# First expert's tokens chosen alone on token-major scores, the others' inside the expert stage; modulation sums on VectorE; new pads in the expert pool

## The chip, the core and the metric

One core of a Trainium2 chip runs the kernel. The metric is the device time of one execution in microseconds; it is the median of several executions. PE is the TensorE matmul queue, PEld its weight loads, DVE is VectorE, ACT is ScalarE, POOL is GpSimd and SP is SyncE, which here only issues DMAs.

## The reference

One layer of a transformer block on 2048 tokens of width 1024, in float32. What the change touches:

```python
mod = silu(c) @ w_ada + b_ada                 # 6 rows of 1024: sh1, sc1, g1, sh2, sc2, g2
h = ln(x) * (1 + sc1) + sh1                   # modulated input
y = token_mixer(h @ w_in, ...)                # convolution branch + two-way retention, gated, @ w_out
x = layer_norm(ALPHA * x + g1 * y)
h = ln(x) * (1 + sc2) + sh2
aff = softmax(h @ w_router)                   # 2048 tokens x 16 experts
gates, idx = top_k(aff.T, 256)                # each expert takes its 256 best tokens
xe = h[idx]                                   # 16 x 256 x 1024
he = silu(xe @ w_gate) * (xe @ w_up)
ye = (he @ w_down) * gates                    # added back at idx
x = layer_norm(ALPHA * x + g2 * sum(ye))
```

## The kernel before

All products are float32 by three matmuls: each operand is split into a rounded high part and the rest (`split`, lines 78 to 85: ACT makes the high part at L80, DVE, or POOL on request, subtracts at L81), and `mm3` (L87 to L89) multiplies high by high, high by low and low by high. Raw weights come by DMA into four "raw" buffers of 512 KB, and the split weights stand in a ring of 24 "w" slots.

The program runs in stages. First the modulation rows sh1 and sc1 are made (`first_modulation`), then the in-projection goes in two halves of the tokens over groups of output columns (U, K, Q, V, G, GA, GB), with the 31-tap convolution on DVE as a filler (`cacc`, L466). Then come retention, the mixing of the two branches with the router (`affs`, the 2048 x 16 scores, made at L860), the choice of each expert's tokens, and 16 experts. An expert has four steps f2 of gate and up products (32 products of 128x256 in each step) and then 32 down products of 128x512.

**Modulation.** `ada_rows` (L237) makes sc2, sh2, g1 and g2 from 1024x1024 pieces of `w_ada`: `ada_k` puts plain float32 matmuls (L199) of a 32-column stationary `crep` on PE. Rounds 0 and 1 (g1, sh2; sc2) are a generator that `fillers2` pumps, one step after each pair of token tiles of half 0 from group 6 on (`pump(1, fillers2)`). Round 2 (g2) is pumped between the counts of the search (`g2fill`); its two 2 MB loads (`wg2`, L929) borrow the places of the expert tiles heT and xeT.

**Search.** The scores are transposed so that each expert has 8 partitions of 256 tokens (`seg`). All 16 thresholds are then found together, two bits a round, in 15 rounds: three compares with counting on DVE (L953), a matmul that adds up the 8 partitions (L956), and two small steps (L967, L971). Ties and ranks follow (L981 to L1006, ending in `pin`, each token's place in each expert's list), then expert 0's list by one-hot products (L1040 to L1058, `idx`), its gather on POOL (`x_gather`, L1075), the transposes and splits of its 256 token rows (`x_prep`), and the lists of experts 0 to 3 (`make_lists(0)`, matmuls `ix` at L1024).

**What sets the order.** A scheduler orders each engine's queue by the place in the program and by its own estimates; `tc.issue_after` ties a step to an instruction. The weights of expert 0's first three steps (`first`, L914) are loaded and split ahead, with the subtraction on POOL. Within the expert stage the gather of expert e+1 stands at the start of expert e and its `x_prep` after step f2 = 1. Two small tiles `pad0` and `pad1` (24 and 8 floats, L927) stand ahead of heT and xeT in the pool.

Of the kernel before, what the change touches and what calls it, by code (L numbers as in the profile page):

```python
# [42 lines left out]
def body(ctx: ExitStack, tc: tile.TileContext, x, ctxt, cc, w_ada0, w_ada, b_row, b_col, w_in, conv_w, conv_b,  # L43
         conv_g, conv_bb, w_conv, lgf, lgb, gn_g, w_ret, w_out, ln1_g, ln1_b, w_router,
         w_gate, w_up, w_down, ln2_g, ln2_b, k_rope, k_pos, k_dif, k_sel, k_iota, k_bits, out):
# [144 lines left out]
    def ada_k(crep, c0, ps, k, halves=2, pre=None):  # L190
        for half in range(halves):
            if pre is not None:
                wt = pre[k // 4][:, k % 4]
            else:
                wt = raw(f"wa{c0}_{k}_{half}", [P, D])
                nc.sync.dma_start(wt, w_ada[c0 // D - 2 + half, k])
            for j in range(2):
                jj = half * 2 + j
                T.matmul(ps[32 * jj:32 * jj + 32, :], crep[:, k], wt[:, j * 512:(j + 1) * 512],  # L199
                         start=k == 0, stop=k == KD - 1)  # L200
                if pre is not None:
                    yield
        if pre is None:
            yield

# [31 lines left out]
    def ada_rows(crep, rnd, halves, tmp, pre=None):  # L237
        c0 = 2048 * (rnd + 1) if rnd < 2 else 5120
        n = 2 * halves

        def load_b():
            br = tmp("br")
            for j in range(n):
                nc.sync.dma_start(br[32 * j:32 * j + 32], bass.AP(tensor=b_row.tensor, offset=b_row.offset + c0 + 512 * j,
                                                                  ap=[[0, 32], [1, 512]]))
            return br

        ps = u_ps(f"ada{rnd + 1}")
        br = load_b() if pre is not None else None
        for k in range(KD):  # L250
            yield from ada_k(crep, c0, ps, k, halves, pre)
        mr = tmp("mr")
        if br is None:
            br = load_b()
        V.tensor_tensor(mr[:32 * n], ps[:32 * n], br[:32 * n], ALU.add)
        for j in range(n):
            r = c0 // 512 - 4 + j
            nc.sync.dma_start(d_mod[r:r + 1], mr[32 * j:32 * j + 1])
        yield
# [412 lines left out]
    for half in range(2):  # L672
        pairs = [half * 4 + i for i in range(4)]
        for gi, g in enumerate(GROUPS):
# [5 lines left out]
            for pi, pid in enumerate(plist):  # L680
# [107 lines left out]
    digit = const.tile([P, 15, 4], I32, name="digit")  # L788
    nc.scalar.dma_start(digit, k_bits)
    sameb = const.tile([P, P], BF16, name="sameb")  # L790
    kst = r2k("kst")
    nc.scalar.dma_start(kst[:, :P], k_sel[:, 1])
    V.tensor_copy(sameb, kst[:, :P])
# [113 lines left out]
    iota16, tokid, blk, iota128 = kio[:, 0:16], kio[:, 16:32], kio[:, 32:40], kio[:, 40:168]  # L907
# [16 lines left out]
    same, low = ksel[:, 0], ksel[:, 1]  # L924
    wg2 = []
# [4 lines left out]
    g2fill = [ada_rows(rep_c(ep)[0], 2, 1, lambda name: e4k(name, [P, 512]), wg2)]  # L930
    with tc.issue_after(pows[0].ins), tc.issue_after(exps[0].ins):
        first = [[gu_slabs(w[0], f2, True) for w in (w_gate, w_up)] for f2 in range(3)]
    segb = e2k("seg")
    seg = segb[:, :256]
    ps = tr_ps()
    for a in range(2):
        T.transpose(ps[:, a * P:(a + 1) * P], affs[:, a].rearrange("p s e -> p (s e)"), ident)
    V.tensor_copy(seg, ps[:, :256])
    seg16 = ep.tile([P, 256], BF16, name="seg16", tag="tk_seg16", bufs=1)
    V.tensor_copy(seg16, seg.bitcast(BF16).rearrange("p (n two) -> p n two", two=2)[:, :, 1])  # L940

    dps = mm_ps("dps").bitcast(I32)
    digp = dps[:, 0:60].rearrange("p (i c) -> p i c", c=4)
    nxp = dps[:, 64:124].rearrange("p (i c) -> p i c", c=4)
    V.tensor_copy(dps[:, 0:60], digit.rearrange("p i c -> p (i c)"))
    cand = tk("cand", 4, I32, 2)
    V.tensor_copy(cand, digp[:, 14])
    for i in range(14, -1, -1):
        cnt = tk("cnt", 3, BF16, 2)
        for j in range(3):  # L950
            junk = e2k("junk")
            junk = junk[:, :128].bitcast(BF16) if i >= 8 else junk[:, :256]
            V.tensor_scalar(junk, seg16 if i >= 8 else seg, cand[:, j + 1:j + 2].bitcast(F32), 0.0,  # L953
                            op0=ALU.is_ge, op1=ALU.add, accum_out=cnt[:, j:j + 1])
        pc = u_ps("cnt")
        cmm = T.matmul(pc[:, 0:3], sameb, cnt, start=True, stop=True)  # L956
        if i < 14:
            with tc.issue_after(cmm.ins):
                pump(1, g2fill)
        hits = tk("hits", 3, F32, 2)  # L960
        dig = tk("dig", 1, F32, 2)
        if i > 0:
            nx = nxp[:, i]
            V.tensor_tensor(nx, cand[:, 0:1].to_broadcast([P, 4]), digp[:, i - 1], ALU.bitwise_or)
        else:
            nx = cand[:, 0:1].to_broadcast([P, 4])
        V.tensor_scalar(hits, pc[:, 0:3], CAP - 0.5, 0.0, op0=ALU.is_ge, op1=ALU.add, accum_out=dig)  # L967
        cand = tk("cand", 4, I32, 2)
        if i >= 4:

            V.scalar_tensor_tensor(cand, dig.to_broadcast([P, 4]), float(1 << 2 * i), nx, op0=ALU.mult, op1=ALU.add)  # L971
        else:
            digi = tk("digi", 1, I32, 2)
            V.tensor_scalar(digi, dig, float(1 << 2 * i), None, op0=ALU.mult)
            V.tensor_tensor(cand, digi.to_broadcast([P, 4]), nx, ALU.bitwise_or)
    tb = cand[:, 0:1]
    thr = tb.bitcast(F32)
    ge = e2k("ge")
    gt, eq = ge[:, :256], ge[:, 256:]
    cc2 = tk("cc2", 2)  # L980
    V.tensor_scalar(gt, seg, thr, 0.0, op0=ALU.is_gt, op1=ALU.add, accum_out=cc2[:, 0:1])  # L981
    V.tensor_scalar(eq, seg, thr, 0.0, op0=ALU.is_equal, op1=ALU.add, accum_out=cc2[:, 1:2])
    pc = u_ps("cnt")
    T.matmul(pc[:, 0:1], same, cc2[:, 0:1], start=True, stop=True)
    T.matmul(pc[:, 1:2], low, cc2[:, 1:2], start=True, stop=True)
    lim = tk("lim", 1)
    V.tensor_scalar(lim, pc[:, 0:1], -1.0, float(CAP), op0=ALU.mult, op1=ALU.add)
    V.tensor_tensor(lim, lim, pc[:, 1:2], ALU.subtract)
    oneb = e2k("oneb")
    ones, scn = oneb[:, :256], oneb[:, 256:]  # L990
    V.memset(ones, 1.0)
    V.tensor_tensor_scan(scn, ones, eq, 0.0, op0=ALU.mult, op1=ALU.add)
    selb = e2k("selb")
    sel, sq = selb[:, :256], selb[:, 256:]
    V.scalar_tensor_tensor(sq, scn, lim, eq, op0=ALU.is_le, op1=ALU.mult)
    cs1 = tk("cs1", 1)
    V.scalar_tensor_tensor(sel, gt, 1.0, sq, op0=ALU.mult, op1=ALU.add, accum_out=cs1)
    pc = u_ps("cnt")
    T.matmul(pc[:, 0:1], low, cs1, start=True, stop=True)
    V.tensor_tensor_scan(scn, ones, sel, 0.0, op0=ALU.mult, op1=ALU.add)  # L1000
    V.scalar_tensor_tensor(sq, scn, pc[:, 0:1], sel, op0=ALU.add, op1=ALU.mult)
    ps = tr_ps()
    for a in range(2):
        T.transpose(ps[:, a * P:(a + 1) * P], sq[:, a * P:(a + 1) * P], ident)
    pin = tk("pin", 256, I32)
    V.tensor_scalar(pin, ps[:, :256], -1.0, None, op0=ALU.add)  # L1006
    def make_lists(gq):
        e0 = gq * 4
        px = u_ps("ix")
        n = 0  # L1010
        for a in range(2):
            for s0 in range(0, 8, 4):
                oa = ep.tile([P, 256], F32R, name="oa", tag="e2k", bufs=6)
                ob = ep.tile([P, 2, 256], F32R, name="ob", tag="e2k", bufs=6)
                for off, dst in ((0, oa), (256, ob[:, 0])):
                    src = pabf[:, off + a * P + s0 * NE:off + a * P + (s0 + 4) * NE].rearrange("p (s e) -> p s e", s=4)[:, :, e0:e0 + 4]
# [21 lines left out]
    pin0 = pin.rearrange("p (a s e) -> p a s e", a=2, s=8)[:, :, :, 0]  # L1038
    pt = tk("pt", 32, I32)
    V.tensor_scalar(pt[:, 0:16].rearrange("p (s a) -> p a s", a=2), pin0, P - 1, None, op0=ALU.bitwise_and)  # L1040
# [22 lines left out]
    V.tensor_scalar(pa, pin, 4, None, op0=ALU.arith_shift_right)  # L1063
    V.tensor_scalar(pb, pin, 15, None, op0=ALU.bitwise_and)
    pabf = e2k("pabf")
    V.tensor_copy(pabf, pab)

# [221 lines left out]
```

## Time and profile before

| | us |
|---|---|
| median of 3 runs | 3068.63 (3064.36 to 3070.91) |
| the profiled execution | 3070.69 |
| its span (first to last instruction) | 3068.9 |
| PE busy | 2978.8 (97%) |
| DVE busy | 2114.8 (69%) |
| ACT busy | 1158.3 (38%) |
| POOL busy | 361.2 (12%) |
| DMA | 560.25 MB, 183 GB/s |

About 1.8 us lie around the span. The profiled execution is 2.06 us above the median. Durations in what follows are of this one execution. Matmuls are pipelined, so the row of a matmul is longer than the distance to the next one: the cost of a matmul on a full PE is the distance from its start to the next start. PE's mean granted clock is 0.988 of full speed.

### The profile page before, as it was taken

Reading aid. Unit: us, or ns where it says so; the run is one execution under the profiler, and the core shown is the slowest. Engines: PE = TensorE matmul, PEld = TensorE weight load, DVE = VectorE, ACT = ScalarE, POOL = GpSimd, SP = SyncE. Lnnn points to the kernel's source line nnn. Section 1 sums busy time; section 2 is a strip of 40 time slices with the busy share of each in tenths; the row PEclk is TensorE's granted clock in tenths of the full one; section 3 lists DMA queues with packets and bytes.
Section 4 is the critical chain, followed back from the end, with each engine's and each line's share of the span. In section 5 each row is a group of like instructions: output and inputs, shape, how many; then the busy total and the mean of one; then the engine's idle time right before and its main releaser. Section 6 shows DMA issues by size and latency. Waiting matters only on the chain. (4 is left out here: it accounts for less than half of the span.)

```text
span 3068.9 us, 47411 instructions
## 1 busy us (share of the span) xinstructions
PE 2978.8 (97%) x18089; PEld 2603.1 (85%) x18089; DVE 2114.8 (69%) x3898; ACT 1158.3 (38%) x2110; POOL 361.2 (12%) x325
## 2 busy tenths in 40 slices
PE   6999999999999999999999996999999999999998
PEld 5988877789888888888878883999999999999987
DVE  4366777442678986888867777566666666568886
ACT  4323122242231333544421112555555555544443
POOL 2100000000000000111101114010100000012331
PEclk9999999999999999999999997999999999999999
DMA  7334455332452334666764445667677667778875
GB/s 249 106 121 172 146 178 173 116 110 82 170 190 82 122 117 144 215 206 206 242 209 152 145 138 183 198 203 206 211 216 215 216 209 211 214 245 269 274 239 202
DMA packets 195044, 560.25 MB, mean 183 GB/s; under 512 B 29064, under 2 KB 44328, under 8 KB 194816
## 3 DMA queue, kind: packets, MB, share of 16 engines
q1 hardware_dynamic: 170272, 486.90, 47.8%
q0 software_dynamic: 18064, 64.62, 7.4%
q10 hardware_dynamic: 6480, 5.70, 0.6%
q8 instruction: 142, 2.33, 0.3%
q14 instruction: 86, 0.70, 0.1%
HBM read 429.24 MB, written 127.89 MB: 182 GB/s over the span
## 5 line engine op out<-in xcount | busy, mean ns | idle before, releaser
L87 PE MATMUL mm<-xeT,sg 128*128 128x256 f32 x2048 | 577.0, 282 | 0.0
L89 PE MATMUL mm<-xeT,sg 128*128 128x256 f32 x2048 | 575.6, 281 | 1.2 <-DVE sg L81 1.2
L88 PE MATMUL mm<-xeT,sg 128*128 128x256 f32 x2048 | 575.5, 281 | 0.0
L81 DVE TENSOR_TENSOR sg<-rg,sg 128x512 fp32r<-128x512 f32 x488 | 329.8, 690 | 249.2 <-ACT sg L80 244.5
L80 ACT ACTIVATE sg<-rg 128x512 fp32r<-128x512 f32 x512 | 313.5, 629 | 321.8 <-PE mm L89 222.6
L89 PEld LDWEIGHTS mm<-xeT,sg 128*128 128x128 f32 x2048 | 386.1, 189 | 1.4 <-DVE sg L81 1.4
L88 PEld LDWEIGHTS mm<-xeT,sg 128*128 128x128 f32 x2048 | 386.2, 189 | 0.7
L87 PEld LDWEIGHTS mm<-xeT,sg 128*128 128x128 f32 x2048 | 385.9, 189 | 0.7
L466 DVE SCALAR_TENSOR_TENSOR cacc<-yw,cvw,cacc 128x384 f32<-128x384 f32 (+1 forms) x600 | 376.8, 641 | 8.7
L81 DVE TENSOR_TENSOR sd<-rd,sd 128x512 fp32r<-128x512 f32 x256 | 172.6, 688 | 89.9 <-ACT sd L80 89.1
L80 ACT ACTIVATE sd<-rd 128x512 fp32r<-128x512 f32 x256 | 157.2, 629 | 135.3 <-PE mm L89 88.3
L88 PE MATMUL mm<-sd,heT 128*128 128x512 f32 x512 | 203.0, 397 | 3.7 <-DVE sd L81 3.7
L89 PE MATMUL mm<-sd,heT 128*128 128x512 f32 x512 | 203.1, 397 | 1.9 <-DVE heT L81 1.9
L87 PE MATMUL mm<-sd,heT 128*128 128x512 f32 x512 | 203.1, 397 | 1.4 <-ACT heT L80 1.4
L154 POOL TENSOR_TENSOR rs<-rs,mhalf 128x1 f32<-128x1 f32 (+1 forms) x50 | 37.6, 752 | 1294.1 <-DVE rs L153 1278.1
L87 PE MATMUL mm<-hT,sU 128*128 128x256 f32 x512 | 146.1, 288 | 4.4 <-ACT us L707 2.2
L88 PE MATMUL mm<-hT,sU 128*128 128x256 f32 x512 | 146.0, 286 | 0.0
L89 PE MATMUL mm<-hT,sU 128*128 128x256 f32 x512 | 145.1, 285 | 0.0
L147 POOL TENSOR_TENSOR rs<-rs,mhalf 128x1 f32<-128x1 f32 x58 | 86.6, 1493 | 365.9 <-DVE rs L146 365.7
L88 PEld LDWEIGHTS mm<-sd,heT 128*128 128x128 f32 x512 | 96.7, 189 | 27.4 <-DVE sd L81 5.4
L89 PEld LDWEIGHTS mm<-sd,heT 128*128 128x128 f32 x512 | 96.6, 189 | 25.9 <-DVE heT L81 3.1
L443 ACT ACTIVATE gs<-mm 128x512 f32<-128x512 f32 x96 | 54.9, 597 | 168.2 <-PE mm L89 133.0
(357 smaller groups left out, 7073.7 us busy)
## 6 DMA issues: line engine op xcount, KB each, us to landing
rg<-w_gate SPq DMA_DIRECT2D x128, 512.0 KB
rg<-w_up SPq DMA_DIRECT2D x128, 512.0 KB
rd<-w_down SPq DMA_DIRECT2D x128, 512.0 KB
wa<-w_ada SPq DMA_DIRECT2D x40, 512.0 KB
d_v<-vs SPq DMA_DIRECT2D x32, 512.0 KB
vsr<-d_v SPq DMA_DIRECT2D x32, 512.0 KB
xt<-x SPq DMA_DIRECT2D x16, 512.0 KB
rU<-w_in SPq DMA_DIRECT2D x16, 512.0 KB
```

The costliest lines, as they stand in the source:

```text
L80: A.activation(hi, src, AF.Copy)
L81: eng.tensor_tensor(lo, src, hi.bitcast(F32), ALU.subtract)
L87: T.matmul(ps, s[0], m[0], start=start, stop=False)
L88: T.matmul(ps, s[0], m[1], start=False, stop=False)
L89: return T.matmul(ps, s[1], m[0], start=False, stop=stop_)
L147: pows[0] = G.tensor_tensor(rs, rs, mhalf[:, :1], ALU.pow)
L154: G.tensor_tensor(rs[:, 0], rs[:, 0], mhalf[:, :heads], ALU.pow)
L443: A.activation(s, ps, AF.Sigmoid)
L466: V.scalar_tensor_tensor(acc[:, :n], y[:, tap:tap + n], cvw[:, cgp, tap:tap + 1], acc[:, :n], op0=ALU.mult, op1=ALU.add)
```

## The change

It has four parts.

1. `ada_rows` and `ada_k` are replaced by `ada_sums`: for each of g1, sh2, sc2 and g2, DVE multiplies 8 loaded pieces of 128x1024 by the activated conditioning vector and adds them up (8 instructions of 128x1024), then two float32 matmuls of 8x512 with `mhalf` (filled with -0.5) add over the partitions, and two small DVE steps multiply by -2 and add the bias. All four are pumped in half 0 of the in-projection, two steps after every odd pair. g2 is no longer made in the search, and the 2 MB loads there are gone.
2. `choose(e0, n, nb, ...)` replaces the common search. It works on the scores as they come out of the router, tokens on partitions, 16 of them for each expert in a partition. A round decides nb bits: one compare of 16 x n x (2^nb - 1), one reduction over the 16, one matmul with a matrix of ones, and the small steps. Expert 0 alone is searched ahead of its gather, with 4 bits a round in 8 rounds, on tiles in PSUM.
3. Experts 1 to 3 are chosen inside expert 0, 4 to 7 inside experts 1 and 2, 8 to 11 inside 3 and 4, 12 to 15 inside 5 and 6, with 3 bits a round in 10 rounds, pumped after every 6th product (expert 0) or every 16th (later). `make_lists` follows each; the gather of expert 1 comes after the first lists (f2 = 2 of expert 0), and its `x_prep` after f2 = 3.
4. The pads are now 56 and 24 floats. The constants of the search that are gone and new ones (`digit` 240 B and `sameb` 256 B out, `iota16` 64 B and `onesb` 256 B in) make the constant pool 192 bytes a partition smaller, so that all tiles behind it move. In the compiled programs the w slots, hT and most large tiles start at 0 modulo 256 bytes before and at 64 now; heT at 128 before and at 64 now; xeT at 160 before and at 96 now. Measured from the w slots, heT goes from 128 to 0 and xeT from 160 to 32.

```diff
-    def ada_k(crep, c0, ps, k, halves=2, pre=None):
...
-                T.matmul(ps[32 * jj:32 * jj + 32, :], crep[:, k], wt[:, j * 512:(j + 1) * 512],
-                         start=k == 0, stop=k == KD - 1)
-    def ada_rows(crep, rnd, halves, tmp, pre=None):
...
+    def ada_sums(c0, tmp):
+        acc = ip.tile([P, D], F32, name="acc", tag="t4k", bufs=3)
         for k in range(KD):
-            yield from ada_k(crep, c0, ps, k, halves, pre)
+            wt = raw(f"wa{c0}_{k}", [P, D])
+            nc.sync.dma_start(wt, w_ada[c0 // D - 2, k])
+            if k == 0:
+                V.tensor_scalar(acc, wt, sg[:, k, 0:1], None, op0=ALU.mult)
+            else:
+                V.scalar_tensor_tensor(acc, wt, sg[:, k, 0:1], acc, op0=ALU.mult, op1=ALU.add)
+            yield
...
+            T.matmul(ps[c], mhalf, acc[:, j * 512:(j + 1) * 512], start=True, stop=True)
...
                 if half == 0 and gi > 5:
-                    pump(1, fillers2)
+                    pump(2 if pi % 2 else 1, fillers2)
...
-                fillers2.append(ada_rows(crep, 0, 2, t2k))
-                fillers2.append(ada_rows(crep, 1, 1, t2k))
+                fillers2.extend(ada_sums(c0, t2k) for c0 in (2048, 3072, 4096, 5120))
...
-    for i, (tag, bufs) in enumerate((("heT", 1), ("xeT", 2))):
-        V.memset(ep.tile([P, (24, 8)[i]], F32, name=f"pad{i}"), 0.0)
-        wg2.append(ep.tile([P, 4, D], F32, name="wg2", tag=tag, bufs=bufs))
-        nc.sync.dma_start(wg2[i], w_ada[3, i * 4:i * 4 + 4].rearrange("k p f -> p k f"))
...
+    place(56)
+    heT0 = ep.tile([P, KD, 2, 256], F32R, name="heT", tag="heT", bufs=1)
+    place(24)
...
+        for r, sh in enumerate(shifts):
+            m = J[r] - 1
+            cm = cmps[:, :n * m * 16].rearrange("p (e j t) -> p e j t", e=n, j=m)
+            V.tensor_tensor(cm, v[:, :, None, :].to_broadcast([P, n, m, 16]),
+                            thr[:, :, 1:, None].bitcast(F32).to_broadcast([P, n, m, 16]), ALU.is_ge)
...
+                V.tensor_reduce(cnt.rearrange("p (e j) -> p e j", e=n), cm, axis=AX.X, op=ALU.add)
...
+            yield
+            pc = u_ps("cnt")
+            T.matmul(pc[:, :n * m], onesb, cnt, start=True, stop=True)
...
+    for _ in choose(0, 1, 4, pins[:, 0:1], fast):
+        pass
...
+        xes = x_gather(e + 1) if 0 < e < NE - 1 else None
+        if e in (0, 1, 3, 5):
+            gq = (e + 1) // 2
+            selfill.append(choose(max(4 * gq, 1), 4 if gq else 3, 3, pins[:, 0 if gq else 1:]))
...
+                        products += 1
+                        if products % 6 == 0 if e == 0 else products % 16 == 0:
+                            with tc.issue_after(done.ins):
+                                pump(1, selfill)
...
+            if e == 0 and f2 == 2 or e in (2, 4, 6) and f2 == 3:
+                pump(1000, selfill)
+                make_lists(e // 2)
+                if e == 0:
+                    xes = x_gather(1)
+            if f2 == (1 if e else 3) and e + 1 < NE:
                 nxt = x_prep(e + 1, xes)
```

The order of DVE's queue from the last scores on, before: `seg` is the transposed scores, `cand` the candidate thresholds, `junk` the compare's output.

```order
L860 TENSOR_TENSOR affs<-sx,mx 128x2x2x16
L938 COPY seg<-tr 128x256
L940 COPY seg_17285<-seg 128x256
L953 TENSOR_SCALAR junk,cnt<-seg_17285,cand 128x256 x3
L967 TENSOR_SCALAR hits,dig<-cnt 128x3
L971 SCALAR_TENSOR_TENSOR cand<-dig,dps 128x4
```

The same place now: `dps` holds expert 0's scores and the thresholds in PSUM, `cw` the work tile of the search.

```order
L842 TENSOR_TENSOR affs<-sx,mx 128x2x2x16
L937 COPY dps<-affs 128x16
L962 TENSOR_TENSOR cw<-dps,cw 128x240
L966 TENSOR_REDUCE cw<-cw 128x15
L981 TENSOR_SCALAR cw<-cnt 128x15
L992 SCALAR_TENSOR_TENSOR cw<-cw,dps 128x16
```

Each round had three compares and has one compare and one reduction. After two rounds a scaling of `g2r` (128x1024, L1158 now) stands in this queue too, which stood behind the list of expert 0.

POOL's queue before, from the last small steps of the mixing stage: `sg` are the slots of expert 0's first three steps, `xe` a gathered tile of 128 tokens.

```order
L147 TENSOR_TENSOR rs_17081<-rs_17081,mhalf 128x1
L81 TENSOR_TENSOR sg<-rg,sg 128x512 x24
L1075 DMA xe<-d_h_260,idx 128x1040 x7
L1221 DMA d_acc<-ye,idx 2048x1024 x2
L1075 DMA xe<-d_h_260,idx 128x1040 x2
```

POOL's queue now:

```order
L147 TENSOR_TENSOR rs_17107<-rs_17107,mhalf 128x1
L81 TENSOR_TENSOR sg<-rg,sg 128x512 x24
L1100 DMA xe<-d_h_260,idx 128x1040 x7
L1256 DMA d_acc<-ye,idx 2048x1024 x2
L1100 DMA xe<-d_h_260,idx 128x1040
```

All 24 subtractions stand ahead of expert 0's gather in both.

PE's queue at the start of expert 0, before: `ix` are the list matmuls of experts 0 to 3.

```order
L160 MATMUL tr<-ident,xe 128x128 x4
L1024 MATMUL ix<-ob,oa 64x64 x2
L87 MATMUL mm<-xeT,sg 128x256
L1024 MATMUL ix<-ob,oa 64x64
L87 MATMUL mm<-xeT,sg 128x256 x3
```

PE's queue now, the last matmuls ahead of expert 0's first product:

```order
L1015 MATMUL rank<-cr,ksel 128x16
L1091 MATMUL ix_17401<-mv_17398,oh 128x2 x16
L160 MATMUL tr<-ident,xe 128x128 x16
L87 MATMUL mm<-xeT,sg 128x256 x4
```

and at the first count of the choice for experts 1 to 3, some 35 matmuls later:

```order
L89 MATMUL mm<-xeT,sg 128x256
L978 LDWEIGHTS onesb
L978 MATMUL cnt<-cw,onesb 128x21
L87 MATMUL mm<-xeT,sg 128x256
```

The next counts follow about 22 matmuls apart.

## Rows read from the trace of the kernel before

**Rows 1.** Windows: PE, PEld, DVE, ACT, POOL busy, clock, DMA share, GB/s.

```profile
390.00:650.00 260.00, 260.00 (x1198) 201.57 (x1197) 154.97 (x305) 71.42 (x129) 8.22 (x14) 1.00 0.45 151
2100.00:2600.00 500.00, 499.59 (x3582) 469.29 (x3581) 313.29 (x469) 268.23 (x460) 37.91 (x28) 1.00 0.70 212
1922.00:1924.00 2.00, 1.81 (x12) 1.68 (x10) 0.69 (x1) 1.25 (x4) 0.00 (x0) 0.50 0.30 123
```

**Rows 2.** Timeline, the search and the first expert's start: start, length, instruction.

```profile
1870.62 0.23 DVE L860 TENSOR_TENSOR affs<-sx,mx 128x64 f32<-128x64 f32 x1
...
1870.72 9.88 POOL L81 TENSOR_TENSOR sg<-rg,sg 128x512 fp32r<-128x512 f32 x8 [9.97 <-ACT sg L80]
...
1874.79 0.16 PE L956 MATMUL cnt<-cnt,sameb 128*128 128x3 bf16 x1 [3.20 <-DVE junk L953]
...
1875.39 0.48 DVE L953 TENSOR_SCALAR_CACHE_REDUCE junk<-seg,cand 128x256 bf16<-128x256 bf16 x1
...
1884.79 19.68 POOL L81 TENSOR_TENSOR sg<-rg,sg 128x512 fp32r<-128x512 f32 x16 [4.20 <-ACT sg L80]
...
1903.46 0.16 PE L956 MATMUL cnt<-cnt,sameb 128*128 128x3 bf16 x1
...
1910.56 0.42 DVE L1006 TENSOR_SCALAR pin<-tr 128x256 int32<-128x256 f32 x1 [0.78 <-PE tr L1004]
...
1916.99 1.08 POOL L1075 DMA_INDIRECT xe<-d_h,idx  x1 [12.52 <-DVE idx L1058]
...
1921.41 1.97 PE L160 MATMUL tr<-ident,xe 128*128 128x128 f32 x8 [2.05 <-DMA xe<-d_h,idx]
...
1925.75 0.38 PE L87 MATMUL mm<-xeT,sg 128*128 128x256 f32 x1
```

**Rows 3.** Timeline of PE around one modulation pump.

```profile
402.62 0.39 PE L89 MATMUL mm<-sG,hT 128*128 128x512 f32 x1
402.94 1.06 PE L199 MATMUL ada<-wa,crep 128*32 128x512 f32 x8
403.93 0.50 PE L87 MATMUL mm<-sG,hT 128*128 128x512 f32 x1
```

**Rows 4.** Tile wa, 380 to 640 us: median ns, first and last start.

```profile
L199 PE MATMUL ada<-wa,crep x96: 592/605/617, 390.8 to 589.0; 128*32 128x512 f32 x96
```

**Rows 5.** Lines of DVE, 1600 to 1870 us: busy us, mean ns.

```profile
L824 DVE SCALAR_TENSOR_TENSOR h<-xl,mv,sc2r 128x1024 f32<-128x1024 f32 x15 | 19.1, 1276 | 0.0
```

**Rows 6.** Timeline of PE: two small float32 matmuls in the search.

```profile
1906.26 0.36 PE L985 MATMUL cnt<-cc,ksel 128*128 128x1 f32 x2
```

**Rows 7.** Timeline: the last list matmul among products, and expert 1's gather.

```profile
1927.08 0.36 PE L88 MATMUL mm<-xeT,sg 128*128 128x256 f32 x1
...
1927.28 0.19 PE L1024 MATMUL ix<-ob,oa 128*64 128x64 f32 x1
...
1927.31 0.36 PE L89 MATMUL mm<-xeT,sg 128*128 128x256 f32 x1
...
1933.18 0.94 POOL L1075 DMA_INDIRECT xe<-d_h,idx  x1 [13.82 <-PE mm L89]
```

**Rows 8.** Timeline of PE: first rows of unbroken runs of products, and of what follows.

```profile
693.71 0.36 PE L87 MATMUL mm<-hT,sU 128*128 128x256 f32 x1
...
768.30 0.40 PE L87 MATMUL mm<-sK,hT 128*128 128x512 f32 x1
...
1051.61 0.39 PE L87 MATMUL mm<-sGA,hT 128*128 128x512 f32 x1
...
1084.26 0.60 PE L475 MATMUL tr<-ident,cacc 128*128 128x128 f32 x4
...
1974.03 0.40 PE L87 MATMUL mm<-sd,heT 128*128 128x512 f32 x1
...
1996.33 0.28 PE L87 MATMUL mm<-xeT,sg 128*128 128x256 f32 x1
...
2019.12 0.48 PE L1024 MATMUL ix<-ob,oa 128*64 128x64 f32 x6
```

More of the change, by code (lines that the diff above doesn't have):

```diff
@@ L44, in body @@
          conv_g, conv_bb, w_conv, lgf, lgb, gn_g, w_ret, w_out, ln1_g, ln1_b, w_router,
[L45 removed]
+         w_gate, w_up, w_down, ln2_g, ln2_b, k_rope, k_pos, k_dif, k_sel, k_iota, out):
     nc = tc.nc
@@ L188, in modulation @@
         return modq[k // 2][:, s, k % 2, which:which + 1]
-    def ada_k(crep, c0, ps, k, halves=2, pre=None):
[L191 to L198, printed above, removed]
-                T.matmul(ps[32 * jj:32 * jj + 32, :], crep[:, k], wt[:, j * 512:(j + 1) * 512],
-                         start=k == 0, stop=k == KD - 1)
[L201 to L204, printed above, removed]
     dect = const.tile([P, 10, HEADS], F32, name="dect")
@@ L235, in first_modulation @@
                         ALU.add)
-    def ada_rows(crep, rnd, halves, tmp, pre=None):
[L238 to L249, printed above, removed]
-        for k in range(KD):
-            yield from ada_k(crep, c0, ps, k, halves, pre)
-        mr = tmp("mr")
[L253 to L256, printed above, removed]
+    def ada_sums(c0, tmp):
+        acc = ip.tile([P, D], F32, name="acc", tag="t4k", bufs=3)
+        for k in range(KD):
+            wt = raw(f"wa{c0}_{k}", [P, D])
[5 more added lines that the diff above has]
+            yield
+        ps = u_ps(f"ada{c0}")
+        br = tmp("br")
+        mr = tmp("mr")
+        for j in range(2):
+            c = slice(32 * j, 32 * j + 8)
+            nc.sync.dma_start(br[c], bass.AP(tensor=b_row.tensor, offset=b_row.offset + c0 + 512 * j, ap=[[0, 8], [1, 512]]))
+            T.matmul(ps[c], mhalf, acc[:, j * 512:(j + 1) * 512], start=True, stop=True)
+        for j in range(2):
+            c = slice(32 * j, 32 * j + 8)
+            V.scalar_tensor_tensor(mr[c], ps[c], -2.0, br[c], op0=ALU.mult, op1=ALU.add)
             r = c0 // 512 - 4 + j
@@ L931, in body, with place @@
+    nc.scalar.dma_start(g2r, rows_bc(modr, D, 3072))
+    def place(n):
+        V.memset(ep.tile([P, n], F32, name=f"pad{n}"), 0.0)
+    place(56)
+    heT0 = ep.tile([P, KD, 2, 256], F32R, name="heT", tag="heT", bufs=1)
+    place(24)
     with tc.issue_after(pows[0].ins), tc.issue_after(exps[0].ins):
         first = [[gu_slabs(w[0], f2, True) for w in (w_gate, w_up)] for f2 in range(3)]
[L933 to L937, printed above, removed]
@@ L948, in body @@
[L948 to L964, printed above, removed]
-        else:
[L966 to L987, printed above, removed]
@@ new lines, in body @@
+    pin = tk("pin", 64, I32)
+    pins = pin.rearrange("p (e t) -> p e t", e=4)
+    fast = mm_ps("dps")
+    for r, sh in enumerate((26, 22, 18, 14, 10, 6, 2, 0)):
+        V.tensor_scalar(fast[:, 64 + 16 * r:64 + 16 * (r + 1)].bitcast(I32), iota16, float(1 << sh), None, op0=ALU.mult)
+    for _ in choose(0, 1, 4, pins[:, 0:1], fast):
+        pass
+    def make_lists(gq):
+        pab = ep.tile([P, 512], I32, name="pab", tag="e2k", bufs=6)
+        V.tensor_scalar(pab[:, 0:64], pin, 4, None, op0=ALU.arith_shift_right)
+        V.tensor_scalar(pab[:, 64:128], pin, 15, None, op0=ALU.bitwise_and)
+        pabf = e2k("pabf")
+        V.tensor_copy(pabf[:, :128], pab[:, :128])
@@ L1014, in make_lists @@
                 ob = ep.tile([P, 2, 256], F32R, name="ob", tag="e2k", bufs=6)
-                for off, dst in ((0, oa), (256, ob[:, 0])):
-                    src = pabf[:, off + a * P + s0 * NE:off + a * P + (s0 + 4) * NE].rearrange("p (s e) -> p s e", s=4)[:, :, e0:e0 + 4]
+                for off, dst in ((0, oa), (64, ob[:, 0])):
+                    src = pabf[:, off:off + 64].rearrange("p (e s a) -> p s e a", e=4, a=2)[:, s0:s0 + 4, :, a]
                     V.tensor_tensor(dst.rearrange("p (s e q) -> p s e q", s=4, e=4),
@@ L1058, in body @@
     V.tensor_copy(idx[:, 0:2], px[:, 0:2])
-    pump(100, g2fill)
-    nc.scalar.dma_start(g2r, rows_bc(modr, D, 3072))
-    pab = ep.tile([P, 512], I32, name="pab", tag="e2k", bufs=6)
-    pa, pb = pab[:, :256], pab[:, 256:]
[L1063 to L1066, printed above, removed]
     def x_gather(e):
@@ L1130, in body @@
     FIN = 11
-    efill = []
+    efill, selfill = [], []
     nxt = x_prep(0, x_gather(0))
-    make_lists(0)
     V.tensor_scalar(g2r, g2r, 1.0 / ALPHA, None, op0=ALU.mult)
+    products = 0
     for e in range(NE):
```

152 lines of the change are left out of this document (100 added, 52 removed).

## The prediction

> **What bounds the kernel now.** I read the views in this order. First the windows, for which engine is full where. In the expert stage from 2100 to 2600 us PE is busy 499.59 of 500 us and DVE 313.29 of 500; in half 0 of the in-projection, where the modulation is pumped, PE is busy 260.00 of 260 and DVE 154.97 [rows 1]. So in both stages a matmul taken out shortens the time by its share of PE, one put in lengthens it, and DVE has room: 105 us in the one stretch, 187 us in the other. Second the timeline of the one place where PE isn't full, from the last scores at 1870.62 to expert 0's first product at 1925.75 [rows 2]. There the chain of waits is DVE's and POOL's, and every microsecond off it is a microsecond off the end. Third, runs of equal matmuls, for what one really costs on a full PE [rows 8].
>
> The profiled execution is 3070.69 us, 2.06 above the median; the sum is made against it. About 0.2% (6.1 us) is what a measurement of this kernel can tell from no change.
>
> **Part 1, modulation sums.** The pump shown sits between a product at 402.62 and one at 403.93, that is 1.31 us where products otherwise start 0.227 apart, so it costs 1.08 us [rows 3, 8]. There are 16 such pumps (96 records, eight of 8 and eight of 4, all between 390.8 and 589.0 [rows 4]); a smaller one loads half as much but switches the form of the matmul as often, so I take 1.1 for each: 17.6 us leave PE. Four pairs of 8x512 matmuls come in. Nothing like them is in the trace; the nearest row is the pump, so 1.1 each, 4.4 us (0.5 to 1.1 each). Net 13 us faster. On DVE it adds 4 x 8 instructions of 128x1024 at up to 1.28 [rows 5], 41 us, into 105 us of idle time: hidden. The uncertainty is order, not volume. DVE now waits for each of the 32 loads of `wa` in its own queue; behind a late load stand the evictions of gates and the convolution, and behind those PE, whose PSUM buffers fill. Eight loads more also pass through SP and the four raw buffers, but the DMA share there is 0.45 [rows 1]. Ends: 18 us faster, and no gain if DVE loses 13 us to loads.
>
> **Part 2, the search for expert 0.** Now: 15 rounds from the first count at 1874.79 to the last at 1903.46, 28.67 / 14 = 2.05 us each; then 7.1 us to `pin`, 6.4 to the gather, 4.4 until its rows have landed (1916.99 to 1921.41), 4.3 to the first product [rows 2]. After: a round has the 0.60 us from a count to the next compare (1874.79 to 1875.39), one compare and one reduction over 240 elements. No such reduction is in the trace; I take the compare of 256 elements, 0.48 [rows 2], for both: 1.56 us, 8 rounds 12.5 us (a reduction at half or double that would make it 10.5 to 16). From 1870.85 that is 1883.6 with the first copy; ties and ranks on 16 elements instead of 256 I take at half of 7.1, the list without the modulation's 0.7 us at 5.7. So `idx` would be ready near 1893, 24 us earlier.
>
> But the gather is not free to go then. On POOL it stands behind all 24 subtractions of `first`, as the order shows. Those took 9.88 us for 8 and 19.68 us for 16, with 4.20 us of waiting for weights between [rows 2]; the waiting goes with the two 2 MB loads, which were in flight then. 29.6 us from 1870.72 end at 1900.3, so the gather starts near 1900.5 instead of 1916.99: 16.5 us earlier, and everything behind it. Ends: 12 us, if the 4.2 us of waiting stay; 24 us, if POOL runs ahead of this. The first products were already at half clock when they came (granted 0.50 at 1922 to 1924 [rows 1]), though matmuls of the modulation had run between the counts; so their absence in the search costs nothing new, or 2 us at most.
>
> **Part 3, choosing the other experts.** This is new work on a full PE. It issues 40 counts and 20 rank matmuls. The nearest row of a small matmul among products: 1927.08 to 1927.31, 0.23 us where products start 0.12 apart, so 0.11 us [rows 7]. A count also loads its matrix and is bf16, so 0.2 (0.1 to 0.3), 8 us. The rank matmuls are full float32; two with one column took 0.36 us [rows 6], so 0.3 each (0.1 to 0.4), 6 us. The 16 list matmuls of experts 1 to 3 now all stand inside the products, 1 us more. Then stalls: in expert 0 about 22 matmuls, 2.6 us, lie between two counts, while DVE has a compare, a reduction, four small steps and one or two splits to do between them, 2.3 to 5 us by the lengths above and the 0.69 of a split. Some counts come late; I take 3 us in all (0 to 8). Last, expert 1's tokens: from the last list matmul to the gather took 5.9 us [rows 7] and the landing 4.4, in all over 10 us, while about 53 matmuls of gate, up and down lie between in the new order, some 9.5 us; 2 us of stall (0 to 6). Sum 20 us slower, ends 7 and 35. The DVE work itself, about 16 us an expert in some 70, has room behind 313 of 500, and the 24 slots ahead of PE take its bursts.
>
> **Part 4, addresses.** In unbroken runs 96 down products take 22.30 us, 232.3 ns each; 144 products of the same shape in the in-projection take 32.65 us, 226.7 each; 192 gate and up products 22.79 us, 118.7 each; 621 products of the same shape in the in-projection 74.59 us, 120.1 each [rows 8]. The in-projection's operands both start at 0 modulo 256 bytes, down's at 0 and 128, gate and up's at 160 and 0. I read the 5.6 ns as a matter of how the two operands lie to each other. Down's now lie as the in-projection's do: 1536 x 5.6 = 8.6 us faster (0 to 9). Gate and up go to a difference of 32 that no row shows: I take no change, with ends of 8.6 us either way (6144 x 1.4 ns). The Trainium skill says otherwise in TensorE: Matmul & The Clock Gate, Step-by-step: the streaming and the loaded operand have SBUF read ports of their own, so a weight load takes no bandwidth from a running matmul. By that no address would matter and the sum would be 8.6 us worse; the rows above differ by 5.6 ns at equal shape, which that sentence doesn't explain.
>
> **Sum.** -13 - 16.5 + 20 - 8.6 = -18 us on 3070.7, which is 3052.6, or 3050.5 on the scale of the median. I give 3050.
>
> **Rivals.**
> - *Addresses don't matter* (the two rates come from something else, such as the writes that run beside the experts' products). For it: the rates of gate and up go the other way. Time 3050 + 8.6 = 3059, still faster. It is the skill's rule above as a mechanism of this kernel.
> - *POOL does not hold the gather, or the selection costs PE only its lowest price.* 7.5 us more from the search or 12 less in part 3: about 3035 to 3043. For it: the subtractions might run shorter beside a DVE that reads PSUM. Against: in the rows they keep one length all along.
> - *The selection stalls PE.* If counts wait a full DVE turn, and expert 1's `x_prep` is late, part 3 costs 40 instead of 20: 3070, no difference. It decides as soon as DVE's turn between counts passes the 2.6 us of matmuls by 1 us in most of the 40 rounds. For it: DVE's queue in expert 0 is then full; against: the later experts have 48 matmuls between counts.
> - *The new start of 64 is itself the slow one.* Then down stays at 232.3 and the 5904 other 512-column products, at 0 until now, pay 5.6 ns each: 33 us, so 3050 + 8.6 + 33 = 3092, slower. It decides if the distance to a 256-byte border counts rather than the distance between operands. For it: every fast 512-column run in the trace has both at 0. Against: no row shows such an operand at 64.
>
> **Chances.** The forecast's own case 0.37, addresses idle 0.22, better still 0.18, stalls 0.14, slow start 0.09. Faster by over 0.2% (below 3062.5) takes the first three, which hold 0.77, and loses little: 0.76. Within: 0.13, from the stalls and the unknown ends of part 1. Slower: 0.11. The forecast's own range, from the ends of its terms taken half together, is 3038 to 3064. The range that holds 8 in 10 adds the better and the stalling case, each with some us of its own ends, and leaves out the slow start: 3027 to 3077.
>
> **What would show it.** Right: no matmul of the modulation between 390 and 590 but four pairs of 8 columns, PE still full there; 24 subtractions on POOL without a gap, the gather within 0.5 us behind the last; counts among products with 0.1 to 0.3 us around them; down products 227 apart. Wrong: PE idle in half 0 behind DVE or `wa`; a gather that comes earlier than POOL's last subtraction or later than 1904; gaps in PE before counts of more than 8 us together; 512-column products at 232 in the in-projection; an expert longer than now by more than 3 us from expert 7 on, where nothing was added.

## The result, and the profile after

The changed kernel takes 3049.86 us (median of 4 runs, 3046.35 to 3050.80) against 3069.77 for the kernel before: a ratio of 0.9935, 95% interval 0.9920 to 0.9951, some 20 us faster. The forecast was 3050 in a range of 3027 to 3077. The number is right. Two of its four terms are not, the search and the addresses; their errors cancel in part, and 8 us that no term had take up the rest.

The windows of the changed kernel in the columns of [rows 1]: PE is still full in both stages, DVE has 38 us more in the one and 41 in the other. The last row of each set doesn't compare like with like: 1922 to 1924 in the kernel before lies ahead of its first product at 1925.75, so a row from that product on stands below the three.

```profile
390.00:650.00 260.00, 260.00 (x1184) 212.80 (x1183) 193.13 (x350) 77.45 (x135) 11.92 (x18) 1.00 0.49 166
2100.00:2600.00 500.00, 500.00 (x3602) 468.74 (x3601) 354.00 (x679) 272.90 (x482) 41.10 (x31) 1.00 0.71 215
1902.00:1904.00 2.00, 2.00 (x12) 2.00 (x11) 1.22 (x2) 0.60 (x1) 0.00 (x0) 0.57 0.03 8
```

The kernel before, from its first product on:

```profile
1925.70:1927.70 2.00, 2.00 (x19) 1.93 (x17) 1.58 (x3) 1.46 (x5) 0.00 (x0) 1.00 0.03 8
```

There the granted clock is 1.00 (2.4 GHz). In the changed kernel it is 0.50 (1.2 GHz) from 1859.4 to 1903.7, through the whole search, and seven of the first products start 0.21 us apart instead of 0.12: some 0.7 us.

The time goes like this between the two profiled executions (spans 3068.9 and 3049.0). The last scores come at 1859.14 instead of 1870.62: 11.5 us. The in-projection from group G to the start of half 1 gives 14.4. About 2 are lost in the first 150 us, where traces of kernels whose program is the same up to there differ as much (over all runs the first K product starts between 144.9 and 149.6 us). From the last scores to the first product it is 42.8 instead of 55.1 us: 12.3 us. From the first product to the end it is 1147.1 instead of 1143.2: 3.9 us lost.

**The search**, the timeline that answers to [rows 2]. One subtraction run on POOL, 24 long; the ranks and the list on DVE; the gather; the first product:

```profile
1859.14 0.22 DVE L842 TENSOR_TENSOR affs<-sx,mx 128x64 f32<-128x64 f32 x1
...
1859.58 31.31 POOL L81 TENSOR_TENSOR sg<-rg,sg 128x512 fp32r<-128x512 f32 x24 [10.15 <-ACT sg L80]
...
1862.23 1.62 DVE L1158 TENSOR_SCALAR g2r<-g2r 128x1024 f32<-128x1024 f32 x1
...
1866.16 0.41 DVE L966 TENSOR_REDUCE cw<-cw 128x15 bf16<-128x240 bf16 x1
...
1879.39 0.30 DVE L1027 TENSOR_SCALAR pin<-cr 128x16 int32<-128x16 f32 x1
1879.72 1.19 DVE L1074 TENSOR_SCALAR pt<-pin 128x16 int32<-128x16 int32 x1
...
1882.17 1.19 DVE L1077 CAST ptf<-pt 128x32 f32<-128x32 int32 x1
...
1892.99 1.09 POOL L1100 DMA_INDIRECT xe<-d_h,idx  x1 [2.10 <-DVE idx L1092]
...
1897.53 1.97 PE L160 MATMUL tr<-ident,xe 128*128 128x128 f32 x8 [5.02 <-DMA xe<-d_h,idx]
...
1901.94 1.20 PE L87 MATMUL mm<-xeT,sg 128*128 128x256 f32 x4
```

The rounds do what was forecast (a reduction of 240 elements takes 0.41 us, a round 1.53). But the gather doesn't start behind POOL's last subtraction at 1890.89: it waits 2.10 us more, for `idx`. The list between `pin` and the gather took 6.4 us before [rows 2] and takes 13.6. An integer step of 16 elements takes 1.19 us, a conversion of 32 elements 1.19, the scaling of g2r 1.62, where the same forms took 0.18, 0.17 and 0.69 in the kernel before, after POOL had finished:

```profile
1911.02 0.18 DVE L1040 TENSOR_SCALAR pt<-pin 128x16 int32<-128x16 int32 x1
...
1911.79 0.17 DVE L1043 CAST ptf<-pt 128x32 f32<-128x32 int32 x1
```

They stretch to the end of the subtraction that POOL is at. One of POOL's single subtractions, with the DVE step that starts beside it:

```profile
1882.06 1.26 POOL L81 TENSOR_TENSOR sg<-rg,sg 128x512 fp32r<-128x512 f32 x1
...
1882.17 1.19 DVE L1077 CAST ptf<-pt 128x32 f32<-128x32 int32 x1
```

The subtraction ends at 1883.32, the DVE step at 1883.36. From the first scan (1873.87) on, all eight slow steps of 16 or 32 elements end 0.03 to 0.05 us behind one. The larger steps (512 and 1024 elements) hold POOL in turn: four subtractions beside them take 1.7 to 1.8 us instead of 1.26, and the 24 together 31.31 instead of 29.6.

**The expert stage.** A run of 96 down products and the 192 gate and up products behind it, answering to [rows 8]:

```profile
2792.59 0.39 PE L87 MATMUL mm<-sd,heT 128*128 128x512 f32 x1
...
2814.40 0.28 PE L87 MATMUL mm<-xeT,sg 128*128 128x256 f32 x1
...
2836.81 0.71 PE L160 MATMUL tr<-ident,xe 128*128 128x128 f32 x5
```

Down takes 21.81 / 96 = 227.2 ns (232.3 before), gate and up 22.41 / 192 = 116.7 (118.7 before). Products of the in-projection, whose operands now both lie at 64, still start 227 apart (144 in 32.65 us):

```profile
1039.66 0.39 PE L87 MATMUL mm<-sGA,hT 128*128 128x512 f32 x1
...
1072.31 0.60 PE L460 MATMUL tr<-ident,cacc 128*128 128x128 f32 x4
```

A count among the products; expert 1's gather, and PE's wait for its rows:

```profile
2349.27 0.28 PE L89 MATMUL mm<-xeT,sg 128*128 128x256 f32 x1
2349.39 0.19 PE L978 MATMUL cnt<-cw,onesb 128*128 128x28 bf16 x1
2349.43 0.36 PE L87 MATMUL mm<-xeT,sg 128*128 128x256 f32 x1
2349.63 0.28 PE L88 MATMUL mm<-xeT,sg 128*128 128x256 f32 x1
...
1958.19 0.94 POOL L1100 DMA_INDIRECT xe<-d_h,idx  x1 [62.86 <-DMA idx<-d_idx]
...
1963.42 1.09 PE L160 MATMUL tr<-ident,xe 128*128 128x128 f32 x8 [3.23 <-DMA xe<-d_h,idx]
```

From 2349.27 to 2349.63 a count and two products start, 0.36 us where two products take 0.23: 0.13 us for the count.

**The modulation**, tile acc: 32 instructions on DVE and 16 matmul records (four pairs) on PE; 7.9 us of the idle time ahead of DVE's instructions there end with a load.

```profile
L230 DVE SCALAR_TENSOR_TENSOR acc<-wa,sg,acc x28: 1235/1280/1286, 340.3 to 615.4; 128x1024 f32<-128x1024 f32 x28
...
L238 PE MATMUL ada<-acc,mhalf x16: 592/594/597, 449.8 to 655.9; 128*8 128x512 f32 x16
...
  DMA wa<-w_ada: 7.9, 8
```

### The profile page after: what moved, and what is told of

Read it like the earlier page. It is cut to its first block, busy times and chain, and to the rows that moved or that the text cites. A ratio compares the mean times of both kernels' runs of the same rounds, so it can differ in the third digit from the quotient of the medians.

```text
span 3049.0 us, 47645 instructions
## 1 busy us (share of the span) xinstructions
PE 2942.6 (97%) x18050; PEld 2601.5 (85%) x18050; DVE 2213.2 (73%) x4212; ACT 1160.6 (38%) x2110; POOL 370.0 (12%) x325
## 5 line engine op out<-in xcount | busy, mean ns | idle before, releaser
L147 POOL TENSOR_TENSOR rs<-rs,mhalf 128x1 f32<-128x1 f32 x58 | 92.9, 1603 | 369.9 <-DVE rs L146 369.7
```

Of the source, the lines that this page charges most:

```text
L147: pows[0] = G.tensor_tensor(rs, rs, mhalf[:, :1], ALU.pow)
```

## The experiments

The theory after the result: the parts add up, and parts 1 and 4 (sums, offsets) give more than the whole; the split search loses. The rivals: the faster products come from something else in the change, or the expert stage's costs come from the choice's matmuls as priced. Times are medians; the kernel before stood at 3070.2 to 3070.6 in these sets.

**Offsets undone in the changed kernel** (e1).

```diff
-    place(56)
+    place(88)
```

> The changed kernel, but the pad ahead of heT is 32 floats longer: heT and xeT lie again 128 and 160 bytes from the w slots (modulo 256) as before the change, while the slots stay at 64. If the distance between a matmul's two operands sets its rate, down products go from 228.2 back to 233.7 ns and gate and up products from 117.9 to 118.9: 1536 x 5.5 + 6144 x 0.9 ns, 14 us slower than the changed kernel, near 3064. If the rates changed for another reason (the slots' own place at 64, less traffic beside the products), they stay and the time stays near 3050.

Measured: 3067.41 us, ratio to before 0.9987 (0.9977 to 0.9996), 17.5 us slower than the changed kernel. The same run of products there:

```profile
2813.57 0.39 PE L87 MATMUL mm<-sd,heT 128*128 128x512 f32 x1
...
2835.97 0.28 PE L87 MATMUL mm<-xeT,sg 128*128 128x256 f32 x1
...
2858.75 0.71 PE L160 MATMUL tr<-ident,xe 128*128 128x128 f32 x5
```

Down 22.40 / 96 = 233.3 ns, gate and up 22.78 / 192 = 118.6. The w slots stay at 64, the rates go back: the slots' own place doesn't set them. (The longer pad also moves the smaller tiles behind it; of the products' operands only heT and xeT move.)

**Offsets alone in the kernel before** (e3).

```diff
-        V.memset(ep.tile([P, (24, 8)[i]], F32, name=f"pad{i}"), 0.0)
+        V.memset(ep.tile([P, (56, 8)[i]], F32, name=f"pad{i}"), 0.0)
```

> The kernel before, with its first pad 32 floats longer: heT and xeT at 0 and 32 from the w slots, which stay at 0. If the distance counts, down falls from 233.7 to 228.2 ns and gate and up from 118.9 to 117.9, and the kernel before gets 14 us faster, near 3055. If it was something else in the change, the rates stay and the time stays near 3069.

Measured: 3052.82 us, ratio 0.9943 (0.9927 to 0.9960), 17.8 us faster than before, with slots at 0:

```profile
2324.05 0.39 PE L87 MATMUL mm<-sd,heT 128*128 128x512 f32 x1
...
2345.85 0.28 PE L87 MATMUL mm<-xeT,sg 128*128 128x256 f32 x1
...
2368.26 0.49 PE L160 MATMUL tr<-ident,xe 128*128 128x128 f32 x3
```

227.1 and 116.7 ns. One number in one line, and the largest part of the whole change.

**xeT at 0 from the slots** (e2), in the changed kernel.

```diff
-    place(24)
+    place(16)
```

> The changed kernel with the second pad 8 floats shorter: xeT lies at 0 from the w slots instead of 32. The in-projection's products of the same shape, both operands at 0, take 120.1 ns. If the distance alone sets the rate, gate and up go from 117 to 120.1 ns, 6144 x 3 ns, 15 to 19 us slower (near 3067). If only the old 160 was bad, they stay at 117 and the time near 3050.

Measured: 3062.20 us, 12.3 us slower than the changed kernel. The gate and up run:

```profile
2828.30 0.28 PE L87 MATMUL mm<-xeT,sg 128*128 128x256 f32 x1
...
2851.34 0.60 PE L160 MATMUL tr<-ident,xe 128*128 128x128 f32 x4
```

23.04 / 192 = 120.0 ns, the in-projection's rate for this shape [rows 8]. So 0 is good for a product of 512 columns and bad for one of 256. The time rises by less than the 15 to 19 us expected; in this trace the last two experts are 7.0 us shorter than in the changed kernel's (147.7 us to the last product, against 154.7).

**Two more distances** (e10, e11), in the kernel with sums and offsets described below: the first pad 72 floats, then 104.

> The kernel before with the modulation sums and with heT at 64 and xeT at 96 from the w slots (instead of 0 and 32). Known so far: down 226.9 ns at 0 and 232.3 to 233.3 at 128; gate and up 120.2 at 0, 116.9 at 32, 118.2 to 118.9 at 160. If a distance of 0 is down's best and the cost grows with it, down lies between 227 and 233 here; if only whole steps of 128 cost, it stays at 227. For gate and up no theory gives a number; between 116 and 119 the kernel is within 13 us of the one at 0 and 32 (3042).

> As the run before it, with heT at 192 and xeT at 224 from the w slots. If the distance counts in either direction alike (64 behind as 64 ahead), down is as in the run at 64, and gate and up as at 32 (116.9), and the time is that of the kernel at 0 and 32 (3042) plus what down loses, up to 9 us.

Measured: 3062.34 us at 64 and 96, 3048.73 (two runs, 3043.36 and 3054.11) at 192 and 224. The rows of the first, then of the second:

```profile
2316.94 0.40 PE L87 MATMUL mm<-sd,heT 128*128 128x512 f32 x1
...
2339.35 0.28 PE L87 MATMUL mm<-xeT,sg 128*128 128x256 f32 x1
...
2362.37 0.60 PE L160 MATMUL tr<-ident,xe 128*128 128x128 f32 x4
```

```profile
2317.26 0.40 PE L87 MATMUL mm<-sd,heT 128*128 128x512 f32 x1
...
2339.25 0.28 PE L87 MATMUL mm<-xeT,sg 128*128 128x256 f32 x1
...
2361.97 0.49 PE L160 MATMUL tr<-ident,xe 128*128 128x128 f32 x3
```

Down: 233.4 ns at 64, 229.1 at 192. Gate and up: 119.9 at 96, 118.3 at 224. Neither expected shape came out: the cost doesn't grow with the distance (64 is as bad as 128), and 64 ahead and 64 behind differ by 4 ns. Of the distances tried, 0 is best for down and 32 for gate and up. The first of these kernels also settles whether an operand's own place could set the rate. Its heT lies at 64 and its xeT at 96, as in the changed kernel, but its w slots lie at 0 and those of the changed kernel at 64. The same places give 233.4 and 119.9 ns here, 227.2 and 116.7 there: it is the distance to the slots that counts.

**Sums alone in the kernel before** (e5): `ada_sums` in place of `ada_rows`, all four rows in half 0, no `g2fill` and no `wg2`; heT and xeT where they were.

> The kernel before with the modulation sums on VectorE alone (all four rows, g2 among them, so that the search has no matmuls of the modulation and no 2 MB loads); search, lists and pads as before. In-projection: about 14 us faster, as in the changed kernel (the pumps of half 0 gone, four pairs of small matmuls come). Search: if the matmuls of g2 only filled gaps, the rounds stay at 2.05 us; if they delayed the counts, the rounds fall to about 1.9 and 2 us go. If the loads of the modulation held DVE, PE would show waits in half 0 and the gain there would be below 10 us. Expected near 3053 (14 and 2 off 3069).

Measured: 3056.18 us, ratio 0.9954 (0.9937 to 0.9971), 14.4 us faster. The in-projection from G to half 1 gives 14.5 us, the stretch from the router to the first product 1.9, and 2 are lost in the first 150 us, as in the changed kernel. The middle rounds of the search run at 1.94 us, and POOL's 24 subtractions run without a gap (29.91 us), so the wait between them goes with the 2 MB loads. PE shows no wait for DVE in half 0: the loads that DVE waited for held nobody.

**Sums and offsets, the search as before** (e6): the kernel of e5 with a first pad of 56 floats.

> The kernel before with two of the four parts: the modulation sums on VectorE, and heT and xeT at 0 and 32 from the w slots. The search stays common to all experts and ahead of the expert stage. The two parts alone measured 14 and 18 us faster than before. If they add up and the split search (parts 2 and 3) costs more in the expert stage than it saves ahead of it, this is near 3038, some 10 us faster than the whole change (near 3050). If the split search pays as I predicted (16 us saved, 20 paid, so about 4 lost) it is near 3046; if parts 1 and 4 overlap, 3050.

Measured: 3042.33 us, ratio 0.9907 (0.9891 to 0.9924): 28 us faster than before, where the parts alone gave 14.4 and 17.8, and 7.5 us faster than the whole change. The same pair at the old distances, e5 and e1, lies 11.2 us apart the same way. The split search and the choice in the expert stage, taken together, are a loss.

**The third step's subtractions behind the gather** (e4), in the changed kernel.

```diff
-        first = [[gu_slabs(w[0], f2, True) for w in (w_gate, w_up)] for f2 in range(3)]
+        first = [[gu_slabs(w[0], f2, True) for w in (w_gate, w_up)] for f2 in range(2)]
...
     nxt = x_prep(0, x_gather(0))
+    with tc.issue_after(came[0].ins):
+        first.append([gu_slabs(w[0], 2, True) for w in (w_gate, w_up)])
```

(`came[0]` is the first instruction that reads gathered rows.)

> The changed kernel, but the weights of expert 0's third step are loaded and split behind the gather of its tokens instead of ahead of it, so that POOL has 16 subtractions beside the search instead of 24. In the changed kernel the small DVE steps from the ranks on took 0.9 to 1.3 us each while POOL subtracted, against 0.17 before, and the gather waited 2.1 us for the list after POOL's last subtraction. If DVE's steps wait for POOL's instructions, then with POOL done about 10 us earlier (near 1881) the list's steps take 0.2 each again and the gather starts 5 to 8 us earlier, near 1886, and the kernel is 5 to 8 us faster (near 3043). If POOL's queue alone had held the gather, it would start about 2 us earlier or not at all, and if the steps are slow for another reason (cold operands, the PSUM tiles), they stay slow. In both cases the third step's slots could come late; then expert 0 gives it back.

Measured: 3047.14 us, ratio 0.9922 (0.9906 to 0.9939). Its timeline:

```profile
1858.65 20.06 POOL L81 TENSOR_TENSOR sg<-rg,sg 128x512 fp32r<-128x512 f32 x16 [10.76 <-ACT sg L80]
...
1876.34 1.20 DVE L1011 TENSOR_TENSOR_SCAN cr<-cr 128x16 f32<-128x16 f32 x1
...
1878.78 0.17 DVE L1074 TENSOR_SCALAR pt<-pin 128x16 int32<-128x16 int32 x1
...
1879.07 0.18 DVE L1077 CAST ptf<-pt 128x32 f32<-128x32 int32 x1
...
1884.35 1.09 POOL L1100 DMA_INDIRECT xe<-d_h,idx  x1 [5.64 <-DVE idx L1092]
...
1893.48 1.22 PE L87 MATMUL mm<-xeT,sg 128*128 128x256 f32 x4
```

The last of 16 subtractions ends at 1878.71; the scan before that takes 1.20 us, and the list's steps right behind it 0.17 and 0.18, as in the kernel before. The gather starts 8.6 us earlier than in the changed kernel (7.7 counted from the last scores). So DVE was held by POOL's instructions, and POOL's queue was not what held the gather. The end gains less, 2.7 us by the medians, and the runs of the two kernels overlap. Expert 1's rows now come later against PE (PE waits 6.4 us instead of 3.2), and 15 instead of 7 of the first products start 0.21 us apart, not 0.12. Behind the longer wait the granted clock falls. The stretch 1955.10 to 1965.40 here, then in the changed kernel:

```profile
1955.10:1965.40 10.30, 6.11 (x23) 5.35 (x24) 2.57 (x4) 3.12 (x7) 0.94 (x1) 0.50 0.63 219
```

```profile
1955.10:1965.40 10.30, 7.07 (x36) 5.58 (x34) 4.98 (x10) 4.29 (x9) 2.96 (x4) 1.00 0.85 284
```

At 0.50 (1.2 GHz) down products start 0.43 us apart instead of 0.227. Of the 7.1 us by which expert 0 is longer than in the changed kernel some 3 lie there, an estimate from what the waits and the first products leave. The Trainium skill says in GPSIMD Engine Reference, 1. Specifications, that GpSimd shares its SBUF interfaces with VectorE and that DVE instructions with two SBUF inputs, or in a two-port mode, contend. The rows agree as far as they go: the compares of the search, which read PSUM, kept 0.41 us beside POOL in the changed kernel, and so did the bf16 reductions with one input; the scans and integer steps in SBUF took 0.9 to 1.3. Which steps run in a two-port mode no row shows. The price is read from the rows: for a small step, the rest of the subtraction that POOL is at.

**Only the first group chosen** (e8): the choice for experts 4 to 15 is left out, and their lists are made from the places of experts 0 to 3.

```diff
-        if e in (0, 1, 3, 5):
+        if e == 0:
```

> The changed kernel without the choice for experts 4 to 15: their lists are made from the places found for experts 0 to 3, so the output is not the reference's. 30 of the 40 counts, 15 of the 20 rank matmuls and their DVE steps are gone from experts 1 to 6. By the prediction's prices (0.2 and 0.3 us, stalls in part) that is 10 us and more; by the trace of the changed kernel, which has 0.05 us around a count and 0.1 to 0.2 around a rank matmul, it is 3 to 5 us, and the lists' 2.4 us in experts 2, 4 and 6 stay. The stalls of the last two experts (6 us more than before) stay if they come from the order of their own queues, and go if the choice caused them.

Measured: 3038.92 us, 11 us faster than the changed kernel (two runs). But 4.6 us of the difference between the traces stand ahead of the expert stage, where nothing differs but the order that the scheduler found or the execution. Expert 0 is 2.5 us longer (PE waits 4.1 us for expert 1's rows instead of 3.2, and behind that the granted clock is 0.50 for 3.4 us). Experts 1 to 6 together are 6.8 us shorter, between the two expectations: 30 counts at 0.14 and 15 rank matmuls at about 0.2, with the slower start of the product behind each. Of experts 14 and 15, 4.7 us go, but the traces of e2 and e12, which have the whole choice, lack them too, so the choice doesn't always bring them. In the four other traces with the whole choice the two take 163.4 to 166.3 us from their first product to the end of the execution, in all traces without it 159.0 to 162.0; what makes the difference is not shown.

**Expert 1's transposes later** (e9), then **its lists earlier as well** (e12), both in the kernel of e4.

```diff
-            if f2 == (1 if e else 3) and e + 1 < NE:
+            if f2 == 1 and 0 < e < NE - 1:
...
         for n in range(2):
+            if e == 0 and n == 1:
+                nxt = x_prep(1, xes)
```

> The kernel with the third step's subtractions behind the gather (near 3047), and in addition the transposes of expert 1's tokens 18 matmuls (4 us) later, between the two halves of expert 0's down products. There PE waited 6.4 us for expert 1's rows. If that wait is simply the gather's landing, 4 of the 6.4 us go and nothing comes later: near 3043. If the transposes then hold up the start of expert 1, the time stays near 3047.

> The changed kernel with the third step's subtractions behind the gather, expert 1's transposes between the halves of expert 0's down (near 3041.5), and in addition the counts for experts 1 to 3 after every 5th instead of every 6th product, and their lists after the second step instead of the third: in PE's order the last list matmul stands 18 matmuls earlier, so expert 1's gather starts 2 to 4 us earlier. PE waited some 4 us there. If that wait is only the gather's, it goes and the time is near 3038; if DVE can't finish its turns between counts that stand closer, PE waits before the counts instead (it waited 1.3 us in all there), and the time stays at 3041 or rises.

Measured: 3041.50 us (ratio 0.9908, 0.9891 to 0.9924) and 3041.64 (0.9901, 0.9884 to 0.9917). The first came out at the time expected, or a little better, but only in part for the reason given: of the 7.4 us of waits there PE keeps 5.6, now in the middle of the transposes for the split of the first rows, and expert 0 is 3.0 us shorter, also because the granted clock is at 0.50 for 3.4 us there instead of 10. The second brought nothing: PE waits 4.1 us there, but the clock is at 0.50 for 6.8, and expert 0 takes 82.1 us in place of 82.5. The best form of the split search that I found equals the kernel of e6, which doesn't have it. No kernel tried that does the whole computation goes below 3041.

## Why the prediction was right, and where not

- **Part 1, 13 us.** Right: 14.4 on the path. The pumps and the pairs that replace four of them cost about 1.2 us each, not 1.1, as the product behind starts late too; 12 of them net are 14.4. DVE's 39 us lay in idle time, and PE waited for nothing. The 2 us in the search that came with it (e5) weren't in the sum.
- **Part 2, 16.5 us.** Measured 12.3, and 1.9 of these belong to the sums, so 10. The step that failed: "the gather starts near 1900.5", behind POOL's last subtraction. I took POOL as a queue in which the gather stands and priced DVE's list with rows that were recorded after POOL had finished [rows 2]. In the new order the list runs beside POOL and is held by it, 7 us in the list alone; the gather comes 2.1 us behind POOL, and POOL itself ends 2.1 us later after the last scores than forecast, for the most part because DVE's larger steps hold it. The time lay inside my ends, the mechanism was another, and e4 shows it. A warning stood in the trace of the kernel before. There the copy of 256 elements that follows the transposes, from SBUF to SBUF, takes 1.28 us beside a subtraction; the copy of as many elements out of PSUM just ahead of it takes 0.42:

```profile
1871.95 1.27 POOL L81 TENSOR_TENSOR sg<-rg,sg 128x512 fp32r<-128x512 f32 x1
1872.09 1.28 DVE L940 COPY seg<-seg 128x256 bf16<-128x256 bf16 x1
```

A reading of the clock was wrong too: the first products of the kernel before did not come at half clock but at 1.00 (the row from 1925.70 above). The end of 2 us given for it holds: some 0.7 us were lost.
- **Part 3, 20 us.** Against the kernel with the same offsets (e3) experts 0 to 6 cost 16 us more in the changed kernel, 9.0 of it in expert 0. Counts cost 0.14 us each, not 0.2 (from the product ahead to the second one behind, less two products, mean of 40: 5.5 us); rank matmuls about 5 instead of 6; the waits before counts 0.6 us in all, not 3; lists 2; expert 1's rows 3.2 instead of 2. DVE at 354 of 500 us kept up. Price and time are inside the ends of 7 and 35. The 9.0 of expert 0 include the 0.7 us at low clock. In this execution the last two experts added 6 us more, which e2 doesn't have.
- **Part 4, 8.6 us.** The reading of the two rates as the operands' distance was right: of the products' operands e1, e2 and e3 move only heT and xeT, and they move the time by 12 to 18 us; e10 against the changed kernel separates the distance from the places. The Trainium skill (TensorE: Matmul & The Clock Gate, Step-by-step) gives the two operands read ports of their own, and by that alone no distance would matter. The measurement decides against that conclusion; whether it is the ports that the two operands share is not shown. The size was wrong by half. Down gave 8 to 9 us as forecast; "gate and up: I take no change" failed: at 32 they take 116.7 instead of 118.7 ns, 10 to 12 us over 6144, beyond the end of 8.6 us that I had drawn from the nearest row.
- **Rivals.** "Addresses don't matter" and "64 is itself the slow start" are refuted by e1 and by the in-projection's unchanged 227 ns. "The selection stalls PE" did so only at expert 1's rows. "POOL does not hold the gather" came true in its words and not in its sense: the list held it, and it came later, not earlier.
- **The sum.** 14 and 2 us from the sums, 10 from the split search and 18 from the offsets are gained and 16 lost in the expert stage: 28 us. 2 us at the start and 6 in the last experts of this execution leave 20. My 18 hit it by luck: an underrated part 4 and an overrated part 2 cancel in part, and the losses at the start and in the last experts, which were no part of the sum, took the rest.

## What to carry to other kernels

Price a step with rows recorded beside the engines that will run beside it, not only with rows of the same shape: small SBUF steps on DVE took 0.17 us alone and 1.2 beside GpSimd subtractions. Where equal matmuls run at different rates, look at the distance of the operands' addresses modulo 256 bytes and try a few pads per shape before touching the algorithm; here that was worth 18 us of 3070, more than any other part. When a change has several parts, measure each alone: two of four parts gave 28 us, the other two took 8 back.

## What the runs showed that I had not expected

The rate of a product depends on how far apart the moving and the stationary operand start, and not in a simple way. Counted from the w slots to heT or xeT modulo 256 bytes (that 256 is the period is not shown): with 512 moving columns 227.1 ns at a distance of 0, 233.4 at 64, 232.3 to 233.3 at 128, 229.1 at 192; with 256 moving columns 120.0 at 0, 116.7 at 32, 119.9 at 96, 118.6 at 160, 118.3 at 224. What in the chip makes this is not shown by any run. And a DVE step that has nothing to do with POOL's data can be held until the POOL instruction that is running ends, if it works in SBUF alone. Not every such step is. Held were scans, copies, conversions, and integer and elementwise steps of 4 elements and more. Not held were the compares of the kernel before, which have an accumulator (256 elements, 0.48 us beside POOL and after it alike), the bf16 reductions (0.41), and steps on one element (0.15 to 0.24). No experiment here varies the form of a step by itself.
